# Seven products for a fourth pair of every gate, up and odd block, with the small dependent steps held together among the weights' parts

## The chip, the cores and the metric

The kernel runs on one core of a Trainium2 chip. The metric is the device time of one execution in microseconds (us). The engines are TensorE (PE: matmuls, and PEld for its weight loads), VectorE (DVE), ScalarE (ACT), GpSimd (POOL) and SyncE (SP, which issues the DMAs here).

## The reference

One layer of a streaming encoder on 256 tokens of width 2048, in float32, with a hidden width of 5632 in the two feed-forward networks (FFN):

```python
x = x + 0.5 * swiglu(rms_norm(x, ffn1_norm), ffn1_w_gate, ffn1_w_up, ffn1_w_down)
h = rms_norm(x, mix_norm);  proj = h @ w_in
x = x + concat(pool_mixer(...), gla_mixer(...)) @ w_out
x = x + mem_cross_attention(rms_norm(x, xattn_norm), rms_norm(mem, mem_norm), w_q, w_kv, w_o)
x = x + 0.5 * swiglu(rms_norm(x, ffn2_norm), ffn2_w_gate, ffn2_w_up, ffn2_w_down)
return rms_norm(x, final_norm)
# swiglu(h, wg, wu, wd) = (silu(h @ wg) * (h @ wu)) @ wd
```

All weights are read once, so their stream sets the order of all work. The change is to the gate and up products of the two FFNs, and to small steps around them.

## The kernel before, in words

**Units.** The weights come in units of 1 MB, 256 rows by 1024 columns, which is four quarters of 128 x 512 side by side on the partitions. A matmul runs in a fast form of float32 that keeps only part of the mantissa, so each operand is split in two, hi and lo, and a product is three matmuls: hi x hi, hi x lo, lo x hi (`products`, L323). For a unit that means: its DMA lands in one of three `raw` buffers; ScalarE casts it to hi, `wh` (L241); VectorE subtracts to get lo, `wl` (L242); TensorE does 2 token halves x 4 quarters x 3 = 24 matmuls of 128 x 512 into PSUM. This is a *plain* unit.

**Sevens.** A unit that takes part as a 2 x 2 block of a Strassen-like scheme is a *seven*: seven products instead of eight, 21 matmuls (`seven`, L448). VectorE first makes three sums of quarters in a tile `T`, which has one buffer (`add_weights`, L417: one instruction of 1024 columns and two of 512); then the raw quarters 1 to 3 are split into `xh` and `xl` (two buffers each), and T into `wh` and `wl` (three). The token side needs sums too: `Sums.make` adds up x or y parts of a pair of k-tiles in four short steps (L380 to L392) and splits the results (L247 on ScalarE, L248 on VectorE). With `over=True` one of the four sums replaces a part of the activations that nothing else reads, and three are extra.

**Blocks.** `block_s` goes through eight units of 2048 rows for 1024 columns of gate or up. Four PSUM tiles, all that there are, hold its seven sums and the plain quarters. Behind the last seven `combine` (L504 on ScalarE, L505, L506, L509 on VectorE) adds up the product parts of two tiles; behind the last unit `join(1)` and `join(0)` (L518) add the other two. The gate's result goes through SiLU on ScalarE; up's is multiplied in by VectorE (`ev_up`, L774, four instructions per block pair), three units later; eight transposes per half and a split (`turn`, L779 to L787, with PSUM tile `ph`) put the product into `ys`, the input of down. `turn` comes `CLEAR` units after the pair.

**Order.** An FFN is cut into parts `FF_PARTS`: 4, 4 and 3 columns of blocks, in pairs gate and up (the third part's last block has half gate, half up, "odd"), and a product down after each part. FFN 1's first gate block is a `block_t`, all plain units; that leaves ten `block_s` per FFN. Before, three of the eight units of each are sevens: `PAIRS = (0, 2, 4)`, in order 0 to 7. Some down units and those of the two output projections are sevens as well (`Y_PAIRS`), which stays.

`Stream` (L34 to L90) keeps a list of units and of steps between them; `st.op(f, n)` puts a step behind n more units. `emit` prepares the weights AHEAD = 2 units before TensorE's use: for each unit first the *next* unit's T sums (`prepare`), then this unit's split, then the reload of its raw buffer. Within an engine the tile framework chooses the order by a schedule made when the kernel is built; `in_turn` binds the weights' parts to one another in the order they are written, `latest` being the last one on ScalarE and VectorE, and `behind_weights` (L235) lets a step come no earlier than the latest part. A step placed so may still slide behind many later weights' parts.

**Small steps that the change touches.** At the start, x comes in eight chunks, whose transposes (L645) and splits lie between the first units' products (`amid_first`, L653); their squares (`x_squares`) give the norm's factor, `finish_norm` (L261). The memory's norm `mem_norm` (L1139) squares 16 pieces of the memory on ScalarE (L257) at the end of the first output projection, where `fold` (L702) transposes x anew and splits it (L218, L219).

Of the kernel before, what the change touches and what calls it, by code (L numbers as in the profile page):

```python
# [33 lines left out]
class Stream:  # L34
# [30 lines left out]
    def emit(self, load, prepare, split):  # L65
        done, w, late = -1, {}, []
        for u, f in self.items:
            if u is None:
                f()
                continue  # L70
            ahead = min(u, 1) if u < self.FIRST else self.AHEAD
            while done < min(u + ahead, len(self.units) - 1):
                done += 1
                while late:
                    late.pop(0)()
                if done + 1 < len(self.units):
                    prepare(done + 1, self.units[done + 1][2])
                w[done], rest = split(done, self.units[done][1])

                def finish(done=done, rest=rest):  # L80
                    if rest:
                        rest()
                    if done + self.RAW < len(self.units):
                        load(done + self.RAW)

                if rest:
                    late.append(finish)
                else:
                    finish()
            f(*w.pop(u))  # L90


def build(ctx, tc, I, out):
# [97 lines left out]
    def rsqrt(dst, sums, n, w):  # L191
# [14 lines left out]
        nc.vector.reciprocal(out=dst, in_=v)  # L206

# [27 lines left out]
    def behind_weights(f):  # L235

        with tc.issue_after(latest["vector"].ins), tc.issue_after(latest["scalar"].ins):
            f()

# [6 lines left out]
    def split(hi, lo, src):  # L246
        nc.scalar.copy(hi, src)  # L247
        nc.vector.tensor_tensor(out=lo, in0=src, in1=f32(hi), op=ALU.subtract)  # L248

# [11 lines left out]
    def finish_norm(n, spread_too=True):  # L261

        nc.vector.tensor_reduce(out=sums, in_=ss[:, :, :n], axis=AX.X, op=ALU.add)
        rsqrt(Rcol, sums, D, 2)
        if spread_too:
            diag["R"] = [diagonal(Rcol[:, t : t + 1]) for t in range(2)]

    def spread_norm():
# [96 lines left out]
    class Sums:  # L365
# [6 lines left out]
        def make(self, g):  # L372
# [19 lines left out]
            nc.vector.tensor_tensor(out=p12, in0=p12, in1=p22, op=ALU.add)  # L392
            split(self.tile[:, i, 0], self.tile[:, i, 1], a[:, 4 - n :])
            if self.over:
                split(act[:, 2 * g, 0, P:], act[:, 2 * g, 1, P:], p11)

# [55 lines left out]
    def block_s(srcs, act, sums, order, evict, merge=None, sevens=None):  # L452
# [47 lines left out]
        def combine():  # L500
# [7 lines left out]
            )  # L508
            nc.vector.tensor_tensor(out=e[:, 3], in0=b[:, 1], in1=e[:, 1], op=ALU.add)  # L509
            if merge is not None:  # L510
                merge(e[:, 2:4], e[:, 0:2])

        def join(j):
# [9 lines left out]
        for g in order:  # L523
            if g in sevens:
                st.unit(srcs[g], unit_s(g), split_seven, add_weights)
                if g == sevens[-1]:
                    st.op(combine)
            else:
                st.unit(srcs[g], unit_p(g))
# [123 lines left out]
    def amid_first(u):  # L653

        for c in ((1,), (2, 3))[u] if u < 2 else (u + 2,):
            if c < 8:
# [46 lines left out]
    def fold(c, gain):  # L703
# [43 lines left out]

    PAIRS = (0, 2, 4)
    CLEAR = PAIRS[-1] + 2

    def ffn(wg, wu, wd, down, amid=None):
        gate = {}
        x_sums = Sums("xe", xs, PAIRS, False)

# [33 lines left out]

        for i, g in enumerate(PAIRS):
            st.op(lambda g=g: behind_weights(lambda: x_sums.make(g)), (5, 7, 8)[i])  # L790
        for lo, n in FF_PARTS:
            whole = n == KT // 4
            for b in range(0, n - 1, 2):
# [7 lines left out]
                block_s(wwide(wu, n0), xs, x_sums, range(8), up.__setitem__)  # L801
                st.op(lambda held=held: held.update(gate))
# [6 lines left out]
            if n % 2:  # L809
                def both(j, c):  # L810
# [3 lines left out]
                    else:  # L814
                        ev_up(0, c)
                block_s(wtwo(wu, wg, (lo + n - 1) * NB), xs, x_sums, range(8), both)
                st.op(lambda n=n: turn(gate[0], 4 * (n - 1)), 1)
# [343 lines left out]
    st.op(mem_in, 2)  # L1161
    st.op(mem_norm, 6)

# [296 lines left out]
```

## Time and profile before

| what | us |
|---|---|
| three runs | 2126.57, 2127.61, 2129.54 (median 2127.61) |
| profiled execution, whole | 2126.7 |
| its span, first to last instruction | 2124.9 |
| matmul time of TensorE in it | 2102.9 |
| VectorE | 1615.6 |
| ScalarE | 1064.0 |

The mean granted clock of TensorE is 0.996 of full speed. In the views, L448 is a seven's line, L323 a plain product's; a row of waits has engine, tile and line, then what it waited for, the sum in us, the number of times and the longest; a row of windows has, for each engine, busy us and the number of instructions, then the granted clock, the DMA engines' share and GB/s; a row of a timeline has start, length, engine, line, operation, tiles and, in brackets, idle time before and who ended it; a row of a group ends in its count, busy us and mean ns, and idle time before it.

### The profile page before, as it was taken

The numbers are of one execution on the slowest core, as the hardware profiler recorded it, in microseconds if no ns is written. First come the engines' busy times: TensorE is split into PE (matmuls) and PEld (weight loads), VectorE is DVE, ScalarE is ACT, GpSimd is POOL, SyncE is SP. The second block draws the span as 40 slices with busy tenths as digits, with TensorE's granted clock in tenths as the row PEclk, the third lists the DMA queues.
The fourth block names the chain that finished last, engine by engine and source line by source line (L and its number), as shares of the span: only waits on it lengthen the run. The fifth ranks groups of instructions, "written<-read, shape, count | busy, mean of one in ns | idle before, by whom it ended". The sixth has DMA issues, their size and how long they took to land.

```text
span 2124.9 us, 24308 instructions
## 1 busy us (share of the span) xinstructions
PE 2102.9 (99%) x9972; PEld 1760.2 (83%) x9972; DVE 1615.6 (76%) x1438; ACT 1064.0 (50%) x954; POOL 14.0 (1%) x40
## 2 busy tenths in 40 slices
PE   9899999999999999999999999999999999999998
PEld 7788888888888888888888888888888888888886
DVE  6797889878885676678656555868978889788864
ACT  6554445544544546455645434555544555445444
POOL 0000000000000000000000000000000000000001
PEclk9999999999999999999999999999999999999999
DMA  7456665566656655557755455655567665676573
GB/s 275 162 198 218 231 222 201 198 212 244 215 201 236 221 165 182 170 173 240 251 189 178 158 159 165 232 201 196 198 219 237 218 202 195 218 237 218 200 256 118
DMA packets 143607, 435.94 MB, mean 205 GB/s; under 512 B 9860, under 2 KB 13544, under 8 KB 143112
## 3 DMA queue, kind: packets, MB, share of 16 engines
q1 hardware_dynamic: 143464, 434.38, 60.5%
q8 instruction: 78, 1.28, 0.2%
q14 instruction: 33, 0.27, 0.0%
q10 hardware_dynamic: 32, 0.01, 0.0%
HBM read 417.58 MB, written 16.78 MB: 204 GB/s over the span
## 4 chain that ended last, share of the span: by engine, by line
PE 96%; ACT 1%; DMA 1%; DVE 1%; issue 1%; SPq 0%; DVEq 0%; ACTq 0%
PE pt L323 51%; PE pt L448 17%; PE pa L308 14%; PE pb L323 6%; PE pe L323 3%; PE ph L784 1%; PE pl L1191 1%; PE pv L1226 1%; ACT wh L241 1%; DMA raw<-in_xattn_w_q 0%; DVE wl L242 0%; DMA x<-in_x 0%; PE px L709 0%; PE pp L910 0%; DMA raw<-in_ffn_w_up 0%
## 5 line engine op out<-in xcount | busy, mean ns | idle before, releaser
L242 DVE TENSOR_TENSOR wl<-raw,wh 128x2048 fp32r<-128x2048 f32 (+2 forms) x304 | 684.8, 2254 | 339.4 <-ACT wh L241 338.7
L241 ACT CAST wh<-raw 128x2048 fp32r<-128x2048 f32 (+2 forms) x304 | 572.5, 1884 | 613.2 <-PE pt L323 340.4
L323 PE MATMUL pt<-wh,xs 128*128 128x512 f32 x1856 | 589.6, 391 | 0.6 <-ACT xs L218 0.6
L323 PE MATMUL pt<-wh,ys 128*128 128x512 f32 x1440 | 449.2, 390 | 0.0
L323 PEld LDWEIGHTS pt<-wh,xs 128*128 128x128 f32 x1856 | 348.8, 188 | 73.0 <-ACT xs L218 1.0
L323 PE MATMUL pt<-wl,xs 128*128 128x512 f32 x928 | 362.3, 390 | 0.0
L308 PE MATMUL pa<-xs,wh 128*128 128x512 f32 x896 | 317.5, 398 | 3.3 <-DVE xs L219 3.3
L323 PEld LDWEIGHTS pt<-wh,ys 128*128 128x128 f32 x1440 | 269.9, 188 | 55.7
L323 PE MATMUL pt<-wl,ys 128*128 128x512 f32 x720 | 280.3, 389 | 0.0
L308 PE MATMUL pa<-xs,wl 128*128 128x256 f32 x896 | 249.2, 281 | 0.0
L241 ACT CAST wh<-T 128x2048 fp32r<-128x2048 f32 x78 | 149.4, 1915 | 132.4 <-PE pt L323 86.6
L323 PEld LDWEIGHTS pt<-wl,xs 128*128 128x128 f32 x928 | 174.6, 188 | 35.8
L308 PEld LDWEIGHTS pa<-xs,wh 128*128 128x128 f32 x896 | 168.1, 188 | 42.2 <-DVE xs L219 3.9
L242 DVE TENSOR_TENSOR wl<-T,wh 128x2048 fp32r<-128x2048 f32 x78 | 178.3, 2286 | 29.6 <-ACT wh L241 29.4
L308 PEld LDWEIGHTS pa<-xs,wl 128*128 128x128 f32 x896 | 169.7, 189 | 1.6 <-issue 0.2
L323 PEld LDWEIGHTS pt<-wl,ys 128*128 128x128 f32 x720 | 135.1, 188 | 28.0
L242 DVE TENSOR_TENSOR xl<-raw,xh 128x1536 fp32r<-128x1536 f32 x78 | 136.6, 1751 | 16.4 <-ACT xh L241 16.4
L241 ACT CAST xh<-raw 128x1536 fp32r<-128x1536 f32 x78 | 115.3, 1478 | 61.8 <-PE pt L448 49.7
L448 PE MATMUL pt<-wh,xe 128*128 128x512 f32 x360 | 125.0, 394 | 4.9 <-ACT xe L247 4.9
L323 PE MATMUL pb<-wh,xs 128*128 128x512 f32 x384 | 121.5, 392 | 0.0
L417 DVE TENSOR_TENSOR T<-raw 128x1024 f32<-128x1024 f32 x78 | 95.4, 1223 | 20.6 <-DMA raw<-in_ffn_w_gate 10.0
L417 DVE TENSOR_TENSOR T<-T,raw 128x512 f32<-128x512 f32 x156 | 107.3, 688 | 3.2
(230 smaller groups left out, 2079.7 us busy)
## 6 DMA issues: line engine op xcount, KB each, us to landing
raw<-in_ffn_w_down SPq DMA_DIRECT2D x88, 1024.0 KB, 5.6
raw<-in_ffn_w_up SPq DMA_DIRECT2D x80, 1024.0 KB, 5.7
raw<-in_ffn_w_gate SPq DMA_DIRECT2D x77, 1024.0 KB, 5.1
raw<-in_w_in SPq DMA_DIRECT2D x32, 1024.0 KB, 5.3
raw<-in_xattn_w_kv SPq DMA_DIRECT2D x32, 1024.0 KB, 5.2
raw<-in_w_out SPq DMA_DIRECT2D x16, 1024.0 KB, 5.5
raw<-in_xattn_w_q SPq DMA_DIRECT2D x16, 1024.0 KB, 5.1
raw<-in_xattn_w_o SPq DMA_DIRECT2D x16, 1024.0 KB, 5.5
```

The source lines that it names most:

```text
L241: in_turn("scalar", lambda: nc.scalar.copy(hi, src))
L242: in_turn("vector", lambda: nc.vector.tensor_tensor(out=lo, in0=src, in1=f32(hi), op=ALU.subtract))
L308: nc.tensor.matmul(o, w, x, start=k == 0 and i == 0, stop=last and i == 1)
L323: nc.tensor.matmul(ps, a, w, start=first and i == 0, stop=last and i == 2)
L417: in_turn("vector", lambda: nc.vector.tensor_tensor(out=o, in0=a, in1=b, op=ALU.add))
L448: nc.tensor.matmul(banks[n], x, w, start=n in fresh and j == 0, stop=n in ends and j == 2)
L784: nc.tensor.transpose(v[:, i, h * P : (h + 1) * P], g[:, h, i * P : (i + 1) * P], ident)
L1191: nc.tensor.matmul(ps[:, t, :M], ys[:, 4 * h + d, a, tok], xa["K"][:, d, b, :], start=i == 0, stop=i == 11,)
L1226: nc.tensor.matmul(ps[:, d, :S], xa["V"][:, m, a, col], xa["PT"][:, m, b, :], start=i == 0, stop=i == 5,)
```

## The change

- `PAIRS` becomes (0, 2, 4, 6) and the order of units in every `block_s` 0, 1, 2, 3, 4, 6, 5, 7: four sevens, four plain units, two sevens one behind another. The sums for x are made with `over=True`.
- `emit` splits a seven before it prepares the next unit, if that is a seven too, since T has one buffer.
- `among_weights` is new: it runs a step behind the latest parts and makes the step's own last instructions the latest, so that later parts of weights come behind the step. It is used for the combine, both kinds of token sums, the fold's splits and the first norm's factor.
- The x sums come 5, 7, 9 and 10 units in; `CLEAR` goes from 6 to 7.
- The start has four more spare transposes behind x chunk 0, x chunk 3 one unit later, and the norm's factor one unit earlier, with a square root and a SiLU on ScalarE around it. `turn_gains` of the later gains moves from unit 22 to 35.
- The memory's squares are spread over four units, all behind the weights' parts, and its factor comes at unit 7.

```diff
@@ emit
-                if done + 1 < len(self.units):
-                    prepare(done + 1, self.units[done + 1][2])
+                after = self.units[done + 1][2] if done + 1 < len(self.units) else None
+                both = after and self.units[done][2]
+                if not both:
+                    prepare(done + 1, after)
                 w[done], rest = split(done, self.units[done][1])
+                if both:
+                    prepare(done + 1, after)
@@
+    def among_weights(f):
+        scalar, vector = behind_weights(f)
+        latest["vector"] = vector
+        if scalar is not None:
+            latest["scalar"] = scalar
@@ block_s
-                    st.op(combine)
+                    st.op(combine if merge else lambda: among_weights(combine))
@@ amid_first
-        for c in ((1,), (2, 3))[u] if u < 2 else (u + 2,):
+        for c in ((1,), (2,), (3, 4))[u] if u < 3 else (u + 2,):
@@ fold
-        for j in range(4):
-            split_scaled(xs, 4 * c + j, v[:, j, :], gcol(gain + 4 * c + j))
+        def parts():
+            for j in range(4):
+                done = split_scaled(xs, 4 * c + j, v[:, j, :], gcol(gain + 4 * c + j))
+            return done
+
+        among_weights(parts)
@@ make_y_sums
-            st.op(lambda g=g: behind_weights(lambda: y_sums.make(g)), after)
+            st.op(lambda g=g: among_weights(lambda: y_sums.make(g)), after)
@@ ffn
-    PAIRS = (0, 2, 4)
-    CLEAR = PAIRS[-1] + 2
+    PAIRS, ORDER = (0, 2, 4, 6), (0, 1, 2, 3, 4, 6, 5, 7)
+    CLEAR = 7
-        x_sums = Sums("xe", xs, PAIRS, False)
+        x_sums = Sums("xe", xs, PAIRS, True)
-            st.op(lambda g=g: behind_weights(lambda: x_sums.make(g)), (5, 7, 8)[i])
+            st.op(lambda g=g: among_weights(lambda: x_sums.make(g)), (5, 7, 9, 10)[i])
@@ the three calls of block_s, alike
-                    block_s(wwide(wg, n0), xs, x_sums, range(8), lambda j, c: ev_gate(j, c, 0))
+                    block_s(wwide(wg, n0), xs, x_sums, ORDER, lambda j, c: ev_gate(j, c, 0))
@@ the start
     st.op(lambda: x_chunk(0))
+    st.op(lambda: spare_transposes(4))
-    st.op(lambda: finish_norm(8, False), 7)
+    def first_factor():
+        nc.scalar.activation(chain[:, 1, 0:2], invc[:, 0:2], AF.Sqrt)
+        done = finish_norm(8, False)
+        return nc.scalar.activation(sums, Rcol, AF.Silu), done
+
+    st.op(lambda: among_weights(first_factor), 6)
-    st.op(lambda: turn_gains(G_MIX, G_END), 22)
+    st.op(lambda: turn_gains(G_MIX, G_END), 35)
@@ the memory
+    def mem_squares(lo, hi):
+        for c in range(lo, hi):
+            row_squares([xa[f"mem{h}"][:, c * S : (c + 1) * S] for h in range(2)], c)
+
     def mem_norm():
-        for c in range(8):
-            row_squares([xa[f"mem{h}"][:, c * S : (c + 1) * S] for h in range(2)], c)
-    st.op(mem_norm, 6)
+    for c in range(4):
+        st.op(lambda c=c: behind_weights(lambda: mem_squares(2 * c, 2 * c + 2)), c + 3)
+    st.op(lambda: behind_weights(mem_norm), 7)
```

Helper functions otherwise only return their last instructions.

More of the change, by code (lines that the diff above doesn't have):

```diff
@@ L205, in rsqrt @@
             nc.vector.tensor_tensor(out=v, in0=v, in1=r, op=ALU.add)
-        nc.vector.reciprocal(out=dst, in_=v)
+        return nc.vector.reciprocal(out=dst, in_=v)
     def diagonal(col):
@@ L237, in behind_weights @@
         with tc.issue_after(latest["vector"].ins), tc.issue_after(latest["scalar"].ins):
-            f()
+            return f()
+    def among_weights(f):
[3 more added lines that the diff above has]
+            latest["scalar"] = scalar
     def split_weights(hi, lo, src):
@@ L246, in split @@
     def split(hi, lo, src):
-        nc.scalar.copy(hi, src)
-        nc.vector.tensor_tensor(out=lo, in0=src, in1=f32(hi), op=ALU.subtract)
+        high = nc.scalar.copy(hi, src)
+        return high, nc.vector.tensor_tensor(out=lo, in0=src, in1=f32(hi), op=ALU.subtract)
     def split_pair(dst, kt, src):
@@ L263, in finish_norm @@
         nc.vector.tensor_reduce(out=sums, in_=ss[:, :, :n], axis=AX.X, op=ALU.add)
-        rsqrt(Rcol, sums, D, 2)
+        done = rsqrt(Rcol, sums, D, 2)
         if spread_too:
             diag["R"] = [diagonal(Rcol[:, t : t + 1]) for t in range(2)]
+        return done
     def spread_norm():
@@ L392, in make @@
             nc.vector.tensor_tensor(out=p12, in0=p12, in1=p22, op=ALU.add)
-            split(self.tile[:, i, 0], self.tile[:, i, 1], a[:, 4 - n :])
+            done = split(self.tile[:, i, 0], self.tile[:, i, 1], a[:, 4 - n :])
             if self.over:
-                split(act[:, 2 * g, 0, P:], act[:, 2 * g, 1, P:], p11)
+                done = split(act[:, 2 * g, 0, P:], act[:, 2 * g, 1, P:], p11)
+            return done
         def parts(self, g):
@@ L508, in combine @@
             )
-            nc.vector.tensor_tensor(out=e[:, 3], in0=b[:, 1], in1=e[:, 1], op=ALU.add)
+            last = nc.vector.tensor_tensor(out=e[:, 3], in0=b[:, 1], in1=e[:, 1], op=ALU.add)
             if merge is not None:
                 merge(e[:, 2:4], e[:, 0:2])
+            return None, last
         def join(j):
@@ L711, in fold @@
                 )
-        for j in range(4):
-            split_scaled(xs, 4 * c + j, v[:, j, :], gcol(gain + 4 * c + j))
+        def parts():
+            for j in range(4):
+                done = split_scaled(xs, 4 * c + j, v[:, j, :], gcol(gain + 4 * c + j))
+            return done
+        among_weights(parts)
         for h in range(2):
@@ L797, in ffn @@
                 else:
-                    block_s(wwide(wg, n0), xs, x_sums, range(8), lambda j, c: ev_gate(j, c, 0))
+                    block_s(wwide(wg, n0), xs, x_sums, ORDER, lambda j, c: ev_gate(j, c, 0))
                 held, up = {}, {}
                 into_down = whole and b
-                block_s(wwide(wu, n0), xs, x_sums, range(8), up.__setitem__)
+                block_s(wwide(wu, n0), xs, x_sums, ORDER, up.__setitem__)
                 st.op(lambda held=held: held.update(gate))
@@ L815, in both @@
                         ev_up(0, c)
-                block_s(wtwo(wu, wg, (lo + n - 1) * NB), xs, x_sums, range(8), both)
+                block_s(wtwo(wu, wg, (lo + n - 1) * NB), xs, x_sums, ORDER, both)
                 st.op(lambda n=n: turn(gate[0], 4 * (n - 1)), 1)
```

## Prediction

> **What bounds the kernel now.** First the page: the busy shares and the chain that ended last.
>
> ```profile
> PE 2102.9 (99%) x9972; PEld 1760.2 (83%) x9972; DVE 1615.6 (76%) x1438; ACT 1064.0 (50%) x954; POOL 14.0 (1%) x40
> PE 96%; ACT 1%; DMA 1%; DVE 1%; issue 1%; SPq 0%; DVEq 0%; ACTq 0%
> ```
>
> TensorE (PE) is busy for 99% of the span and carries 96% of the chain, so removed matmuls come off the time, as long as nothing else becomes late. The second row of reading is TensorE's waits, since they are all that is left besides matmuls:
>
> ```profile
> PE pt L448 <- ACT xe L247: 4.9, 1, 4.9
> PE pa L308 <- DVE xs L219: 3.3, 2, 2.8
> ...
> PE pt L448 <- DVE xl L242: 1.2, 1, 1.2
> PE px L645 <- DMA x<-in_x: 0.7, 1, 0.7
> ```
>
> Each is one event, not a steady loss. All blocks of gate and up after the start run without a gap, which the windows over two blocks with three sevens each, and over the down product that follows them two blocks later, show:
>
> ```profile
> core 0: us, PE busy (x) PEld busy (x) DVE busy (x) ACT busy (x) POOL busy (x), PEclk, DMA share, GB/s
> 320.39:361.87 41.48, 41.48 (x184) 34.35 (x183) 36.38 (x27) 22.16 (x16) 0.00 (x0) 1.00 0.58 203
> 361.87:405.17 43.30, 43.30 (x200) 36.01 (x199) 39.54 (x32) 23.29 (x16) 0.00 (x0) 1.00 0.56 195
> ...
> 446.65:533.42 86.77, 86.77 (x393) 72.08 (x391) 75.93 (x68) 41.88 (x29) 0.00 (x0) 1.00 0.66 230
> ```
>
> The reader is to see how near VectorE (DVE) stands: 36.38 of 41.48 us, and 39.54 of 43.30 us in the block that holds 16 turning transposes (200 PE instructions, not 184).
>
> **The removed products.** The pace of a product comes from the chain of waits:
>
> ```profile
> 470.34 4.76 PE pt L448 x21
> 475.10 27.20 PE pt L323 x120
> ```
>
> 27.20 / 120 = 0.2267 us. A plain unit has 24 products, 5.44 us; a seven has 21, 4.76 us. The change makes one more seven in each of 10 blocks per FFN, two FFNs: 20 x 3 = 60 products, 60 x 0.2267 = **-13.6 us**. The Trainium skill (TensorE: Matmul & The Clock Gate, Back-to-back issue gap) has 215.7 ns for 512 columns; by that figure it would be 12.9 us, and the measured pace decides.
>
> **What each new seven costs VectorE.** Its instructions one behind another, in the timeline around the boundary at 361.87:
>
> ```profile
> 349.44 2.28 DVE L242 TENSOR_TENSOR wl<-raw,wh 128x2048 fp32r<-128x2048 f32 x1
> 351.64 1.75 DVE L242 TENSOR_TENSOR xl<-raw,xh 128x1536 fp32r<-128x1536 f32 x1
> 353.31 0.68 DVE L509 TENSOR_TENSOR sg<-pt,sg 128x512 f32<-128x512 f32 x1
> 353.91 2.28 DVE L242 TENSOR_TENSOR wl<-T,wh 128x2048 fp32r<-128x2048 f32 x1
> 356.77 1.22 DVE L417 TENSOR_TENSOR T<-raw 128x1024 f32<-128x1024 f32 x1 [0.57 <-DMA raw<-in_ffn_w_gate]
> 358.02 1.42 DVE L417 TENSOR_TENSOR T<-T,raw 128x512 f32<-128x512 f32 x2
> 359.36 2.28 DVE L242 TENSOR_TENSOR wl<-raw,wh 128x2048 fp32r<-128x2048 f32 x1
> 361.56 1.22 DVE L518 TENSOR_TENSOR sg<-pt,sg 128x1024 f32<-128x1024 f32 x1
> 362.70 1.75 DVE L242 TENSOR_TENSOR xl<-raw,xh 128x1536 fp32r<-128x1536 f32 x1
> 364.36 1.22 DVE L518 TENSOR_TENSOR sg<-pt,sg 128x1024 f32<-128x1024 f32 x1
> 365.50 2.28 DVE L242 TENSOR_TENSOR wl<-T,wh 128x2048 fp32r<-128x2048 f32 x1
> ```
>
> By distance of starts: wl 2.20 (349.44 to 351.64), xl 1.67, the three sums T 2.59 (356.77 to 359.36), a join 1.14 (361.56 to 362.70). A seven takes 2.59 + 1.67 + 2.21 = 6.47 us of VectorE, a plain unit 2.2: each change of one into the other adds 4.27 us to VectorE and takes 0.68 us from TensorE. For the pair of blocks quoted: VectorE 36.38 + 39.54 + 2 x 4.27 = **84.5 us**, TensorE 41.48 + 43.30 - 2 x 0.68 = **83.4 us**. VectorE has more to do than TensorE in such a pair, where it now has 9 us to spare. In down it keeps 11 us of room (75.93 of 86.77), so a debt never passes from one run of four blocks to the next.
>
> VectorE also waits. A raw buffer is loaded again once its unit is split: above, wl ends at 349.44 + 2.28 = 351.72, and T can start on the reloaded buffer at 356.77, **5.05 us** later. The new order 0, 1, 2, 3, 4, 6, 5, 7 puts fewer instructions between that release and the sum that reads the reload. For the third seven they are xl 1.67 and wl 2.21, 3.88 us: VectorE waits about 1.2 us. For the first seven of the next block, behind two sevens in a row, only the second one's wl and a plain wl, 4.41 us: about 0.65 us.
>
> **Where that reaches TensorE.** The static order of the changed kernel differs at the block boundary. Before, the wl of the new block's second unit (359.36 above) stands ahead of both joins. In the changed kernel it stands behind join 1, the next T's first sum, join 0 and the rest of T; where a turn falls, behind its two ys splits too. Join 0 waits for TensorE's last product. The two further durations:
>
> ```profile
> L774 DVE SCALAR_TENSOR_TENSOR sg<-sg,Rcol,sg 128x512 f32<-128x512 f32 x40 | 27.3, 745 | 0.0
> L248 DVE TENSOR_TENSOR ys<-ph,ys 128x1024 fp32r<-128x1024 f32 x22 | 26.0, 1217 | 4.4 <-ACT ys L247 4.4
> ```
>
> I follow one block with a turn, from where TensorE starts its sixth unit, the second of two sevens in a row (time 0), and let that unit's xl be ready just then. Its nine products of plain parts last 2.04 us, so its wl (2.2) just holds. VectorE: wl of the sixth 2.2, of the seventh 4.4; T of the next block's first unit waits for its buffer until 5.05 and ends at 7.65; wl of the eighth 9.85; the combine (0.6 + 1.14 + 0.6 and a wait for ScalarE, about 2.5) 12.35; xl 14.0, wl 16.2; join 1 17.35; first T sum 18.5; ys 19.65; join 0 20.8; ys 21.9; rest of T 23.25; wl of the second unit **25.45**. TensorE: 4.76 + 2 x 5.44 + 1.8 for the transposes (43.30 - 41.48) = 17.44 for the block's end. The next unit's first PSUM tile is the one join 1 frees (17.35, in time); seven products on, at 19.05, it needs the tile that the first ys split frees: 0.65 us lost. Then join 0's tile is in time; at 22.5 it wants the wl of 25.45, or 0.2 us after: 2.8 us. Together about 3.5, with a semaphore's way for each 3.7 us. Without the debt ahead (buffers landing in time) only the last part is left: end + 0.25 + 1.14 (join 0) + 1.13 (ys) + 1.34 + 2.2 = 6.06 against 4.76 + 0.4 us of cover: 0.9.
>
> There are two such boundaries per FFN (into the up block of the second pair of each run of four): 4 x 3.7 = 14.8 us, lower end 4 x 0.9 = 3.6. In three blocks per FFN the four evictions of L774, 4 x 0.66 = 2.65 us by their starts, stand ahead of the sixth unit's xl: by the same walk it is late by 0.7 us, 6 x 0.7 = 4.2, lower end nothing. I take 14.8 + 4.2 = **+19.0 us**, between 3.6 and 22 (3 us more if the boundaries without a turn lose a little each as well: end + 0.25 + 1.14 + 1.34 + 2.2 = 4.93 stands against 4.76 + 0.2 there). I take the long value because the refill of 5.05 us is a row of this trace and the list is fixed.
>
> **What the small steps give back.** Three waits now stand in the trace; first the clock beside them.
>
> ```profile
> 13.84:17.26 3.42, 2.76 (x17) 2.05 (x17) 3.42 (x4) 3.33 (x8) 0.00 (x0) 1.00 1.11 357
> ...
> 58.22:61.63 3.41, 1.53 (x6) 0.63 (x4) 3.41 (x5) 0.06 (x1) 0.00 (x0) 1.00 0.60 179
> 61.63:65.04 3.41, 0.00 (x0) 0.00 (x0) 2.57 (x5) 0.00 (x0) 0.00 (x0) 0.50 0.98 372
> 65.04:68.46 3.42, 2.60 (x6) 2.12 (x7) 3.30 (x9) 3.24 (x5) 0.00 (x0) 0.50 0.16 63
> 68.46:71.87 3.41, 3.41 (x9) 2.64 (x9) 1.24 (x3) 1.59 (x3) 0.00 (x0) 0.50 0.00 0
> ...
> 1037.84:1041.25 3.41, 0.74 (x4) 0.66 (x5) 2.98 (x4) 3.31 (x14) 0.00 (x0) 1.00 0.19 14
> 1041.25:1044.67 3.42, 3.42 (x14) 3.03 (x13) 1.67 (x9) 2.61 (x4) 0.00 (x0) 0.50 0.79 293
> ```
>
> *FFN 1's start.* The rows of token sums come from the groups by line:
>
> ```profile
> L380 DVE TENSOR_TENSOR j<-xs 128x512 f32<-128x512 f32 x6 | 4.1, 684 | 0.0
> ...
> L387 DVE TENSOR_TENSOR j<-j 128x128 f32<-128x128 f32 x18 | 5.2, 286 | 0.2
> ```
>
> One pair's sums are one instruction of the first kind and four short ones (0.68 + 4 x 0.29 = 1.8 us) with their splits behind. Now the waits: 1.2 (xl) and 4.9 us (the token sums, xe), then about 6.0 us at clock 0.50 until 71.87, 3.0 lost: 9.1 us. The sums are now issued as a group among the weights' parts, and a fourth pair's is added, while VectorE has one seven more per block there as well. So the gain lies between nothing and 9.1; neither end is nearer by a row, I take the middle, **-4.6**.
>
> *The memory's norm.* 2.8 us of wait near 1040, and a window of 3.42 us at 0.50 in which its 14 instructions, four of them short ones, would have taken about 2.0 at the pace of full clock: 2.8 + 1.4 = 4.2 us. There the 16 squares of the memory stand on ScalarE between the fold's splits; in the changed kernel's order the splits come together ahead of the squares, which are spread over four units. **-4.2**, at worst nothing.
>
> *The second x chunk.* It waits 0.7 us for its data; one chunk now comes a unit later: **-0.7**, at worst nothing. The other steps cost nothing I can find: four more spare transposes stand where TensorE waits for x anyway; two table loads and the gains' turning are on ScalarE (50% busy) or three short matmuls; without that cover they would cost some 1 us.
>
> **Sum.** -13.6 + 19.0 - 4.6 - 4.2 - 0.7 = -4.1 us. The durations come from the profiled execution of 2126.7 us, which lies 0.9 below the median of 2127.6: 2122.6 on its scale, **2123.5 us** on the median's.
>
> **Rivals.**
> *A, VectorE keeps up.* Debt does not build: the reload lands within 3.9 us when the sum needs it, and boundaries cost 0.9 each. Then -13.6 + 3.6 - 4.6 - 4.2 - 0.7 = -19.5: 2108.1. For it: the DMA queue is at a 0.56 to 0.66 share only. Against it: 5.05 us above, in the same stretch.
> *B, the clock falls at the four turn boundaries; slower.* The longest piece there is 2.8 us of idle. A window of 3.41 us with 1.53 or 0.74 busy was followed by one at 0.50 (58.22, 1037.84); one with 2.76 busy was not (13.84). If the piece falls in one window, 0.6 is busy and the next is at half pace: 1.7 us lost, and as at 65.04 to 71.87 a second one, 3.4. Four times 2.55 on average is +10.2: -4.1 + 10.2 = +6.1, 2133.7. It decides from about 1.9 us of idle within one window; a piece that a window's edge cuts in halves leaves 2.0 busy in each, between the two cases that the rows show. The Trainium skill (TensorE: Matmul & The Clock Gate, Part 1) lets the rate fall only after a whole idle window of about 3.4 us: by that rule 2.8 us would never do it and B would be worth nothing. The wait of 2.8 us near 1040, which is followed by 0.50, speaks against the rule.
> *C, the start keeps its stall.* The fourth pair's sums and seven eat what the grouping gives: -4.1 + 4.6 = +0.5, 2128.1, no change.
>
> **How the numbers follow.** Forecast 0.38, A 0.30, B 0.23, C 0.09. Bounds of the unknown terms around the forecast reach 2119 to 2129; with A below (its gain at the start full: 2104) and B above (one window each at 1.7: 2130; two each: 2137) the range is **2104 to 2136**. A measurement tells 0.2%, 4.3 us, from no change. Faster: A 0.30 and just over half of the forecast case, 0.20, together 0.50; same: the forecast's rest 0.17, C 0.07, B's edge 0.01, together 0.25; slower: B 0.22, C 0.02, forecast 0.01, together 0.25.
>
> **What would show it.** PE instructions on the page 9972 - 60 + 4 = 9916. In the windows of a gate and up pair DVE near its limit (over 95%) and PE below it. In TensorE's waits a new row <- DVE wl L242 at products of plain units, two long ones per FFN of 2 to 3 us, and smaller ones <- DVE ys and xl; no row for xe over 1 us; none of 2.8 us at L308. A mean clock under 0.996 speaks for B; PE waits below 6 us in all for A. The prediction is wrong if the weights' reload is faster than 5 us in the new order, or if stalls come in every block and not at the turns alone.

## The result and the profile after

The changed kernel takes 2140.18 us (median of 4 runs, 2138.35 to 2141.02) against 2127.53 us of the kernel before: 1.006 times as long, 95% interval 1.0047 to 1.0073. It is 12.7 us slower; 4.0 us faster was forecast. The profiled execution took 2141.0 us, its span is 2138.9 (before 2126.7 and 2124.9). From the page, busy time and the chain:

```profile
PE 2099.3 (98%) x9916; PEld 1746.6 (82%) x9916; DVE 1707.2 (80%) x1538; ACT 1092.8 (51%) x986; POOL 14.1 (1%) x40
PE 69%; DVE 19%; DMA 6%; issue 3%; ACT 3%; SPq 0%; DVEq 0%; ACTq 0%
```

TensorE has the 56 instructions less that were counted, but it carries 69% of the chain, not 96%: VectorE now has 19% of it and the DMAs 6%. TensorE's waits, largest first:

```profile
PE pt L462 <- ACT wh L253: 17.6, 14, 2.2
PE pt L462 <- DVE xs L223: 2.0, 2, 1.8
PE pt L462 <- DVE xl L254: 1.9, 5, 0.7
```

The first row, 14 waits and 17.6 us, is for the hi part of a seven, which ScalarE casts when VectorE's sums are ready. (L462 is the seven's line now; before it was L448, and lines further on have moved likewise.) No wait is left at L321, the memory's norm.

Where the time went shows best stage by stage, in the one profiled execution that each kernel has. Below, a stage lasts from TensorE's first product in it to the first of the next one; the columns are the difference to the kernel before in us, for the changed kernel and for four of the experiments told below.

| stage (length before) | changed | fold_free | three_pairs | four_only | three_fold |
|---|---|---|---|---|---|
| FFN 1, gate and up, first run with the start (186.1) | -1.4 | -2.1 | -5.2 | -2.1 | -4.8 |
| second run of four blocks (167.7) | +3.2 | +3.2 | 0.0 | +2.1 | 0.0 |
| third run of three blocks (126.3) | -0.6 | -0.5 | -0.1 | -1.0 | -0.1 |
| mixer's projection (205.2) | -0.7 | +0.5 | -0.3 | +0.4 | +0.5 |
| first output projection (87.4) | **+6.2** | +0.6 | +6.1 | -0.1 | +0.5 |
| attention with the memory's norm (299.8) | -4.7 | -4.0 | -4.4 | +1.2 | -4.0 |
| second output projection (89.7) | **+4.4** | 0.0 | +4.3 | 0.0 | 0.0 |
| FFN 2, gate and up, first run (171.6) | **+5.2** | +4.3 | 0.0 | +3.0 | 0.0 |
| second run (167.7) | +2.3 | +2.6 | -0.1 | +0.9 | -0.1 |
| third run (126.3) | +0.1 | -0.3 | -0.1 | 0.0 | -0.1 |

The down products are within 0.7 us everywhere. Of a run's 2.0 to 2.7 us of removed products (0.68 for each added seven) nothing, or little, is left in any run of gate and up, and the output projections, in which no product was added or removed, lost 10.5 us.

**Inside a run of gate and up.** The four blocks of FFN 1's second run, by windows from block start to block start:

```profile
core 0: us, PE busy (x) PEld busy (x) DVE busy (x) ACT busy (x) POOL busy (x), PEclk, DMA share, GB/s
277.65:318.60 40.95, 40.95 (x182) 33.93 (x181) 38.28 (x28) 22.15 (x14) 0.00 (x0) 1.00 0.66 227
318.60:359.25 40.65, 40.65 (x182) 33.64 (x180) 37.38 (x28) 23.16 (x17) 0.00 (x0) 1.00 0.56 188
359.25:404.38 45.13, 43.39 (x197) 35.06 (x195) 42.67 (x35) 22.07 (x15) 0.00 (x0) 1.00 0.56 191
404.38:448.54 44.16, 41.83 (x182) 33.75 (x181) 40.29 (x29) 22.39 (x17) 0.00 (x0) 1.00 0.58 207
```

The first two blocks run without a gap and keep their gain (40.95 and 40.65, not 41.48). The third and the fourth have TensorE's gaps, and VectorE at 95% and 91% of the time. VectorE falls behind by block; down sets it right. It is not overloaded on the whole: in the four blocks it is busy for 158.6 us, where TensorE's products and transposes need 165.0 (four times 180 products at 0.2267 us, and 1.8), and in the third and fourth block for 83.0, where TensorE needs 83.4. It is late because its list is fixed and it has to stand idle in it, for 12.3 of the 170.9 us, 7.9 of them for reloads. The boundary at 404.38, where a turn falls, on VectorE:

```profile
385.72 1.75 DVE L254 TENSOR_TENSOR xl<-raw,xh 128x1536 fp32r<-128x1536 f32 x1
...
392.64 1.22 DVE L431 TENSOR_TENSOR T<-raw 128x1024 f32<-128x1024 f32 x1 [0.78 <-DMA raw<-in_ffn_w_up]
...
401.69 2.28 DVE L254 TENSOR_TENSOR wl<-T,wh 128x2048 fp32r<-128x2048 f32 x1
403.89 1.22 DVE L533 TENSOR_TENSOR sg<-pt,sg 128x1024 f32<-128x1024 f32 x1
405.03 1.21 DVE L431 TENSOR_TENSOR T<-raw 128x1024 f32<-128x1024 f32 x1
406.16 1.22 DVE L260 TENSOR_TENSOR ys<-ph,ys 128x1024 fp32r<-128x1024 f32 x1
407.29 1.21 DVE L533 TENSOR_TENSOR sg<-pt,sg 128x1024 f32<-128x1024 f32 x1
408.43 1.21 DVE L260 TENSOR_TENSOR ys<-ph,ys 128x1024 fp32r<-128x1024 f32 x1
409.56 1.41 DVE L431 TENSOR_TENSOR T<-T,raw 128x512 f32<-128x512 f32 x2
410.88 2.28 DVE L254 TENSOR_TENSOR wl<-raw,wh 128x2048 fp32r<-128x2048 f32 x1
```

and what TensorE makes of it:

```profile
404.15 0.48 PE L336 MATMUL pt<-wh,xs 128*128 128x512 f32 x1
405.25 0.47 PE L462 MATMUL pt<-xh,xs 128*128 128x512 f32 x1 [0.63 <-DVE sg L533]
...
407.43 0.50 PE L462 MATMUL pt<-wh,xs 128*128 128x512 f32 x1 [0.32 <-DVE ys L260]
...
413.00 0.50 PE L462 MATMUL pt<-wh,xs 128*128 128x512 f32 x1 [1.39 <-ACT wh L253]
```

The reader sees the forecast walk: the sums wait for the reload, join 1 starts when TensorE is at its last products, and from there VectorE does seven things in a row, until 413.2, before the second unit can go on. By starts of products the three waits are 0.88 + 0.49 + 1.55 = 2.92 us (forecast 3.5 to 3.7). Waits in the brackets are shorter than these gaps, since a product's modelled end reaches into them. The last is booked on ScalarE's cast, which follows the rest of T at 410.97, a product that stands ahead of the plain unit's in TensorE's list; the plain unit's wl is ready in the same moment.

The boundary before it has no turn, and it had been given 0.2 us at most:

```profile
357.26 2.28 DVE L254 TENSOR_TENSOR wl<-T,wh 128x2048 fp32r<-128x2048 f32 x1
359.47 1.22 DVE L533 TENSOR_TENSOR sg<-pt,sg 128x1024 f32<-128x1024 f32 x1
360.60 1.21 DVE L431 TENSOR_TENSOR T<-raw 128x1024 f32<-128x1024 f32 x1
361.73 1.22 DVE L533 TENSOR_TENSOR sg<-pt,sg 128x1024 f32<-128x1024 f32 x1
362.87 1.41 DVE L431 TENSOR_TENSOR T<-T,raw 128x512 f32<-128x512 f32 x2
364.19 2.28 DVE L254 TENSOR_TENSOR wl<-raw,wh 128x2048 fp32r<-128x2048 f32 x1
```

TensorE is done with the block at 359.25. Join 0 could start then; it starts at 361.73, because VectorE is still at the first unit's wl (until 359.5) and then at join 1 and a sum. TensorE stands still for 1.65 us after 364.46.

**In the output projections.** VectorE in the first one of the changed kernel:

```profile
981.31 2.28 DVE L254 TENSOR_TENSOR wl<-T,wh 128x2048 fp32r<-128x2048 f32 x1
987.70 0.48 DVE L223 SCALAR_TENSOR_TENSOR xs<-px,gains,xs 128x256 fp32r<-128x256 f32 x1 [4.11 <-ACT xs L222]
988.73 0.49 DVE L223 SCALAR_TENSOR_TENSOR xs<-px,gains,xs 128x256 fp32r<-128x256 f32 x1 [0.54 <-ACT xs L222]
...
994.25 0.48 DVE L223 SCALAR_TENSOR_TENSOR xs<-px,gains,xs 128x256 fp32r<-128x256 f32 x1 [0.54 <-ACT xs L222]
994.65 1.22 DVE L431 TENSOR_TENSOR T<-raw 128x1024 f32<-128x1024 f32 x1
```

and in the kernel before:

```profile
978.60 2.28 DVE L242 TENSOR_TENSOR wl<-T,wh 128x2048 fp32r<-128x2048 f32 x1
980.91 1.23 DVE L417 TENSOR_TENSOR T<-raw 128x1024 f32<-128x1024 f32 x1
982.17 1.42 DVE L417 TENSOR_TENSOR T<-T,raw 128x512 f32<-128x512 f32 x2
983.51 2.29 DVE L242 TENSOR_TENSOR wl<-raw,wh 128x2048 fp32r<-128x2048 f32 x1
985.71 0.48 DVE L219 SCALAR_TENSOR_TENSOR xs<-px,gains,xs 128x256 fp32r<-128x256 f32 x1
```

Before, the next sums and a plain part are made first, and the fold's splits of x come when their transposes are there. In the changed kernel the next sums are bound behind the eight splits. VectorE stands still for 4.1 us until the first one's transposes are done, and then takes about 1.03 us a split, in turn with ScalarE (987.70 to 988.73), so that T starts at 994.65, 11 us after the wl before it has ended, and TensorE runs dry. Behind the waits follows a window of 3.41 us at half rate in each projection (from 1000.3 and 1389.4 us, last section); eight products in it start 0.43 us apart and not 0.23, so that 3.2 of the 10.5 us are the clock's.

### The profile page after: what moved, and what is told of

Its sections match the earlier page's. It is cut to its first block, busy times and chain, and to the rows that moved or that the text cites. A ratio compares the mean times of both kernels' runs of the same rounds, so it can differ in the third digit from the quotient of the medians.

```text
span 2138.9 us, 24386 instructions
## 1 busy us (share of the span) xinstructions
PE 2099.3 (98%) x9916; PEld 1746.6 (82%) x9916; DVE 1707.2 (80%) x1538; ACT 1092.8 (51%) x986; POOL 14.1 (1%) x40
## 4 chain that ended last, share of the span: by engine, by line
PE 69%; DVE 19%; DMA 6%; issue 3%; ACT 3%; SPq 0%; DVEq 0%; ACTq 0%
PE pt L336 32%; PE pa L321 15%; PE pt L462 9%; DVE wl L254 7%; PE pb L336 6%; DVE T L431 5%; PE pe L336 3%; DMA raw<-in_ffn_w_gate 3%; DMA raw<-in_ffn_w_up 2%; DVE xl L254 2%; ACT wh L253 2%; DVE sg L533 1%; DVE sg L520 1%; DVE sg L793 1%; PE pl L1221 1%
## 5 line engine op out<-in xcount | busy, mean ns | idle before, releaser
L254 DVE TENSOR_TENSOR wl<-raw,wh 128x2048 fp32r<-128x2048 f32 (+2 forms) x284 | 637.9, 2250 | 251.7 <-ACT wh L253 251.1
L253 ACT CAST wh<-raw 128x2048 fp32r<-128x2048 f32 (+2 forms) x284 | 532.4, 1881 | 411.1 <-PE pt L336 216.6
L336 PE MATMUL pt<-wh,xs 128*128 128x512 f32 x1536 | 496.7, 392 | 0.0
L336 PEld LDWEIGHTS pt<-wh,xs 128*128 128x128 f32 x1536 | 288.8, 188 | 59.5 <-ACT wh L253 0.2
L321 PE MATMUL pa<-xs,wh 128*128 128x512 f32 x896 | 315.9, 397 | 0.0
L253 ACT CAST wh<-T 128x2048 fp32r<-128x2048 f32 x98 | 187.5, 1913 | 227.3 <-DVE T L431 186.9
L336 PE MATMUL pt<-wl,xs 128*128 128x512 f32 x768 | 300.8, 392 | 1.1 <-DVE wl L254 1.1
L321 PE MATMUL pa<-xs,wl 128*128 128x256 f32 x896 | 248.5, 281 | 0.0
L254 DVE TENSOR_TENSOR wl<-T,wh 128x2048 fp32r<-128x2048 f32 x98 | 224.0, 2286 | 13.5 <-ACT wh L253 13.2
L321 PEld LDWEIGHTS pa<-xs,wh 128*128 128x128 f32 x896 | 167.6, 188 | 38.1 <-issue 0.3
L253 ACT CAST xh<-raw 128x1536 fp32r<-128x1536 f32 x98 | 145.1, 1480 | 97.9 <-DMA raw<-in_ffn_w_gate 52.7
L254 DVE TENSOR_TENSOR xl<-raw,xh 128x1536 fp32r<-128x1536 f32 x98 | 171.5, 1750 | 5.0 <-ACT xh L253 5.0
L336 PEld LDWEIGHTS pt<-wl,xs 128*128 128x128 f32 x768 | 144.8, 189 | 31.7 <-DVE wl L254 2.0
L321 PEld LDWEIGHTS pa<-xs,wl 128*128 128x128 f32 x896 | 169.1, 189 | 1.7 <-issue 0.2
L462 PE MATMUL pt<-wh,xs 128*128 128x512 f32 x320 | 126.4, 395 | 16.2 <-ACT wh L253 14.9
L462 PE MATMUL pt<-wh,xe 128*128 128x512 f32 x320 | 123.2, 389 | 0.0
```

The source lines that it names most:

```text
L253: in_turn("scalar", lambda: nc.scalar.copy(hi, src))
L254: in_turn("vector", lambda: nc.vector.tensor_tensor(out=lo, in0=src, in1=f32(hi), op=ALU.subtract))
L321: nc.tensor.matmul(o, w, x, start=k == 0 and i == 0, stop=last and i == 1)
L336: nc.tensor.matmul(ps, a, w, start=first and i == 0, stop=last and i == 2)
L462: nc.tensor.matmul(banks[n], x, w, start=n in fresh and j == 0, stop=n in ends and j == 2)
```

## The experiments

They ran beside the kernel before, whose median was 2126.0 to 2126.7 us in the three groups; each ratio has its 95% interval.

**1. The fold's splits.** `fold_free` is the changed kernel with one edit:

```diff
-        among_weights(parts)     # fold
+        parts()
```

> The changed kernel, but the fold's eight splits of x are plain again and bind no weights' part behind them. Theory F (the splits, which wait for the transposes and then alternate between ScalarE and VectorE at 1.03 us a step, hold the next weights' parts back by about 11 us at both output projections): the two projections lose their 6.2 and 4.4 us against the kernel before, 2140.2 - 10.5 = 2129.7, perhaps plus up to 4.2 if the wait at the memory's norm comes back. Rival Y (the token sums of y, bound in the same way, are what holds them): no change, 2140. Either way the gate and up stretches stay as they are, about 8.6 us longer in all than before.

Measured: 2131.67 us, 1.0025 (1.0015 to 1.0034). The projections lose 5.6 of 6.2 and all of 4.4 us, the gain at the memory's norm stays, and gate and up change by 1.4 us in all. Theory F holds within 2 us.

**2. The sums of y.**

```diff
-            st.op(lambda g=g: among_weights(lambda: y_sums.make(g)), after)
+            st.op(lambda g=g: behind_weights(lambda: y_sums.make(g)), after)
```

> The changed kernel, but the token sums of y bind no weights' part behind them, as before the change. Theory F: no change within 1.5 us of 2140. Rival Y: the output projections lose their 10.5 us, 2129.7.

Measured: 2135.33 us, 1.0043 (1.0028 to 1.0058): between the two. The first projection gains 3.1 us, the second nothing. So the bound sums of y have a part in the first projection's loss, on top of the splits; at the second the splits alone do it. Of the 3.1 us some 1.6 are the clock, since the window at half rate is missing in the first projection here, and the rest are shorter waits. This is the least sure of the measurements: four runs, three between 2134.5 and 2136.1 and one at 2140.4.

**3. Three pairs again, all small steps as changed.**

```diff
-    PAIRS, ORDER = (0, 2, 4, 6), (0, 1, 2, 3, 4, 6, 5, 7)
-    CLEAR = 7
+    PAIRS, ORDER = (0, 2, 4), tuple(range(8))
+    CLEAR = 6
-        x_sums = Sums("xe", xs, PAIRS, True)
+        x_sums = Sums("xe", xs, PAIRS, False)
```

and the sums again at 5, 7 and 8.

> The changed kernel with three sevens per block again in the order 0 to 7, turns 6 units later and sums as before; all small steps stay as changed. If four sevens are too many for VectorE (theory V): gate and up run without waits as before the change, so the time is the kernel before plus 10.5 us at the output projections, minus 4.7 at the memory's norm and minus 0.7 at the second projection, plus what the start changes (0 to -5): 2128 to 2133. Rival G (the grouping of the combine and the sums causes the waits in gate and up): the waits stay and the saving of 13.6 us goes, about 2150.

Measured: 2127.55 us, 1.0003 (0.9993 to 1.0013), just under the 2128 to 2133 that were expected. Gate and up are back within 0.1 us of the kernel before in all five runs behind the start; the start itself is 5.2 us shorter. The fourth pair makes the waits there (V), and the small steps make those at the projections.

**4. The fourth pair alone.** The kernel before with `PAIRS`, `ORDER`, `CLEAR`, the sums' places and `emit` of the changed one; no `among_weights`.

> The kernel before with only the fourth pair: pairs 0, 2, 4, 6, the new order, sums made in place, turns 7 units later, the split ahead of the next sums between two sevens; no step is bound among the weights' parts, and the start and the memory's norm are as before. Theory V: the same waits in gate and up as in the changed kernel, output projections as before: 2127.5 + 8.7 = 2136, give or take 4. Rival G: no new waits in gate and up, 2127.5 - 13.6 = 2114.

Measured: 2132.16 us, 1.0025 (1.0015 to 1.0035). V in kind, at the lower end of what was expected: 60 products fewer, and slower. Gate and up are 3.0 us over the kernel before in all; in `fold_free` it is 7.2. So the grouping costs some 4 us there: experiment 9.

**5. Both edits, 1 and 3: three pairs, plain fold.**

> Three sevens per block in the order 0 to 7 with the small steps as changed, but the fold's splits plain. If the two causes add (four sevens in gate and up; the fold's splits bound at the projections), only the gains are left: about 5.2 us at the start, 4.0 at the memory's norm, 0.3 elsewhere, less 0.5 at the second projection: 2126.5 - 9 = 2117.5. Rival: the gain at the memory's norm needs the bound splits, then 2121.5.

Measured: 2118.85 us, 0.9964 (0.995 to 0.9978), faster than both kernels. The two causes add: experiments 1 and 3 took 8.5 and 12.6 us off 2140.2, which makes 2119.1. The gain at the memory's norm does not need the bound splits. TensorE's largest waits are now

```profile
PE pt L462 <- ACT wh L253: 3.8, 3, 1.9
PE pt L336 <- DVE wl L254: 2.6, 1, 2.6
```

and all of these lie in the first 80 us.

**6. Turns earlier.** `fold_free` with `CLEAR = 5`.

> The changed kernel with the fold's splits plain (2131.7 us) and the turns 5 units behind the pair, not 7, so that their two splits of ys stand away from the block's end. Theory T (the ys splits between the joins are what makes the wait at those four boundaries long, 2.9 us each): these fall to the 0.5 to 1.6 us of the boundaries without a turn, 2131.7 - 6.5 = 2125. Rival L (VectorE has too much to do in the pair as a whole, wherever the splits stand): the waits move, 2131.7 within 2 us.

Measured: 2131.72 us, 1.0027 (1.0017 to 1.0036), no change. But it decides nothing: the ys splits stand where they stood, one between the joins and one behind them (405.54 and 407.80 us, join 0 at 406.67). By the program the turn's transposes need the PSUM tile that the combine frees, so an earlier place can't move them ahead of it; in the trace they run from 401.4 us on, and the combine ends at 399.5.

**7. The even order.** `fold_free` with `ORDER = (0, 1, 2, 3, 4, 5, 6, 7)`, four sevens.

> The changed kernel with the fold's splits plain and the four sevens in the order 0 to 7, each followed by a plain unit. Theory R (the reload of a raw buffer, 5.05 us, against 3.88 us of work between its release and the next sums): every seven now waits about 1.2 us on its DMA, four times a block, not once or twice, and VectorE has no room for it: 10 to 40 us longer, 2142 to 2172, with VectorE's waits for the weights' DMA at least doubled from the 32 us of the changed kernel. Rival: the pair of sevens in a row is what makes TensorE wait, and the even order is better: under 2128.

Measured: 2155.26 us, 1.0135 (1.0121 to 1.015). R holds: 23.6 us longer. VectorE's waits for the weights in it

```profile
DVE T L431 <- DMA raw<-in_ffn_w_up: 31.0, 24, 1.6
DVE T L431 <- DMA raw<-in_ffn_w_gate: 27.4, 20, 2.3
```

are 58.4 us, where the changed kernel has

```profile
DVE T L431 <- DMA raw<-in_ffn_w_gate: 17.3, 15, 2.4
DVE T L431 <- DMA raw<-in_ffn_w_up: 15.0, 16, 1.5
```

32.3 us (`fold_free`, which differs in nothing but the order, 31.5): 1.8 times, a little under the doubling expected. Two sevens in a row are the better order here; that the second's work covers part of the reload is the count of the prediction.

**8. The sums of the weights on GpSimd.**

```diff
-            in_turn("vector", lambda: nc.vector.tensor_tensor(out=o, in0=a, in1=b, op=ALU.add))
+            in_turn("pool", lambda: nc.gpsimd.tensor_tensor(out=o, in0=a, in1=b, op=ALU.add))
```

> The changed kernel with the fold's splits plain and the sums T of the weights on GpSimd. It takes 2.6 us of each seven off VectorE: in a pair of blocks 84.5 - 8 x 2.6 = 63.7 us. Theory V (VectorE's load): the waits of gate and up go if GpSimd needs no more than about twice VectorE's time per sum: 2131.7 - 18 = 2114 or less. Rival P: GpSimd is over three times slower or slows VectorE beside it; T then comes too late at the two sevens in a row of every block, and the time grows by 2 to 10 us a block, 2170 to 2330.

Measured: 2277.08 us, 1.0705 (1.069 to 1.072), rival P. The sums take

```profile
L431 POOL TENSOR_TENSOR T<-T,raw 128x512 f32<-128x512 f32 x196 | 391.7, 1998 | 15.4
L431 POOL TENSOR_TENSOR T<-raw 128x1024 f32<-128x1024 f32 x98 | 335.4, 3422 | 1252.7 <-DMA raw<-in_xattn_w_o 353.6 <-DVE wl L254 313.0 <-DMA raw<-in_ffn_w_down 167.5
```

3.42 us and twice 2.00 on average, where VectorE needs 1.22 and twice 0.69: 2.8 times as long, 7.4 us ahead of each seven with one T buffer. The averages hide two cases. With VectorE idle beside them the sums take 2.39 and 1.26 us, and at the longest 4.47 and 3.25. The Trainium skill (GPSIMD Engine Reference, 4.1 Engine selection) has about twice for two inputs; the undisturbed sums agree. And VectorE is slowed in its turn, first here, then in `fold_free`:

```profile
L254 DVE TENSOR_TENSOR xl<-raw,xh 128x1536 fp32r<-128x1536 f32 x98 | 232.7, 2374 | 11.5 <-ACT xh L253 11.3
L254 DVE TENSOR_TENSOR xl<-raw,xh 128x1536 fp32r<-128x1536 f32 x98 | 171.5, 1750 | 17.9 <-ACT xh L253 17.9
```

An xl takes 1.75 us when no sum runs on GpSimd and up to 3.96 beside one, a plain wl up to 4.50 in place of 2.29. So of rival P the second half came true, GpSimd slowing VectorE, and not the three times. VectorE's load can't be moved there in this way, and the run leaves open how much of the waits in gate and up a lighter VectorE would save.

**9. The combine unbound.** `fold_free` with

```diff
-                    st.op(combine if merge else lambda: among_weights(combine))
+                    st.op(combine)
```

> The changed kernel with the fold's splits plain and the combine not bound among the weights' parts. If the binding of the combine is what makes gate and up of the changed kernel 4 us longer than those of the kernel with the fourth pair only: 2131.7 - 4 = 2127.7. Rival (the binding of the sums at the start, or the turns, makes the difference): 2131.7 within 1.5.

Measured: 2128.6 us, 1.0009 (1.0 to 1.0018): 3.1 of the 4 us. Unbound, the steps of the combine and the weights' parts mix: in the second run of FFN 1 the next first unit's xl (397.33 us) comes ahead of the combine's last step (399.00).

**10. Combine and sums of y unbound.**

> As the run with the combine unbound, and the token sums of y unbound too: the best that the fourth pair can do with these small steps. 2127 us; if it were under 2118.8, the fourth pair would pay after all.

Measured: 2129.25 us, 1.001 (1.0001 to 1.0019). That is 10.4 us over three pairs with the plain fold, so the fourth pair does not pay in any of the arrangements tried.

**11. Turns without VectorE.** `fold_free` with

```diff
-            split(ys[:, k : k + 4, 0, :], ys[:, k : k + 4, 1, :], v)
+            nc.scalar.copy(ys[:, k : k + 4, 0, :], v)
+            nc.scalar.copy(ys[:, k : k + 4, 1, :], v)
```

> The changed kernel with the fold's splits plain (2131.7 us), and in the turns the lo part of ys is written by ScalarE as a second copy of the hi part: the lo half of the products' left side in down is then not what it should be, the amount of matmul work is the same. VectorE loses two splits of 1.13 us between the joins at each of the four turn boundaries. Theory T (these splits make that wait long): the wait of 2.94 us there falls by 2 to 2.9, in all -8 to -11.6: 2120 to 2124. Rival L (VectorE's load in the pair is what counts): 2.3 us less out of an overload of about 1 us a pair plus waits; the boundaries without a turn, 0.5 to 1.6 us each, gain as well, beyond -11.6.

Measured: 2127.47 us, 0.9999 (0.999 to 1.0009): 4.2 us less, half of what T expected. The wait at the turn of FFN 1's second run falls from 2.9 to 1.55 us, and now TensorE waits for ScalarE's second copy there. The boundary without a turn ahead of it keeps its wait (1.5 us in `fold_free`, 1.4 here), which speaks against rival L. Theory T has the direction; how much the two splits alone cost stays open between 1.4 and 2.9 us a turn, since the copy brings a wait of its own. FFN 2's first run became 2.4 us longer: there the wait for the copy comes in one piece of 2.2 us (1539.5), and the next window runs at half rate (1541.9, 1.6 us). The profiled execution was the slowest of the ten, so the others may not have this.

**12. Only the sums of x bound.** The kernel before, with `among_weights` for `x_sums.make` and nothing else.

> The kernel before, and nothing but the token sums of x bound among the weights' parts. If that is where the 5 us at the start come from: 2126.3 - 5 = 2121.3. Rival (the chunks' order, the spare transposes and the earlier factor give them): 2126.3 within 1.5.

Measured: 2123.19 us, 0.9984 (0.9975 to 0.9994). The start is 3.5 us shorter, so most of the start's gain is these sums (three pairs with all small steps have 4.8 and 5.2 there); a further 1.5 us came at the memory's norm, by the clock (below).

## Why the prediction was wrong

Two steps failed. The boundaries without a turn were taken to cost nothing, and cost 7.9 us; the fold's splits, bound among the weights' parts, were taken to cost nothing, and cost 9.9. Term by term:

- **Products, -13.6.** Right: 60 fewer, at the same pace; the first two blocks of FFN 1's second run show 0.5 and 0.8 us less.
- **Waits in gate and up, +19.0, at most 22.** Too small: about 28. That is the six runs' sum in the table, +8.7, plus the 13.6 that were removed, plus 5.8 gained in the first 92 us (the 331st product of weights starts at 90.9 us, before at 96.7).
  - At the four turns the walk was right: 2.9 us in three of them and 2.3 in the other, 11.1 in all, where 14.8 was taken. It has a slip besides: 17.44 + 0.65 + 4.76 is 22.85 and not 22.5, so that it should have come to 3.1 to 3.3, which is nearer still.
  - The **step that failed** is the boundaries without a turn: "end + 0.25 + 1.14 + 1.34 + 2.2 = 4.93 stands against 4.76 + 0.2 there". This lets join 0 start when TensorE ends. The walk for the turns starts with VectorE's debt, this one without it, though both are boundaries of the same run. With the debt the same list gives 15.64 us for the block's end, wl of the first unit at 16.2, join 1 at 17.35, the first sum 18.5, join 0 19.65, the rest of T 21.0, wl 23.2 against 20.8 (15.64 + 4.76, and 0.4 of cover as at a turn): 2.4 us. The runs show 2.4 (105.8 us), 1.65 (364.5), 0.5 (622.1), 2.1 (1507), 0.9 (1766) and 0.35 (2023), 7.9 us in all; 0.8 more came two units behind the one at 1507 (1520), and 1.6 through the clock behind the first (109.4). The prediction had named stalls outside the turns as a sign of being wrong.
  - The late xl behind the evictions, for which 4.2 was taken, is five waits of 0.3 to 0.5 us, 2.0 in all. What is left of the 28 us is 1.0 at the start of FFN 2's last down (2061.4), about 0.1 behind each wait, since the second product after one starts 0.33 us after the first and not 0.23 (366.34 and 366.67), and smaller pieces.
  - VectorE's load came out a little smaller than the 84.5 us of the sum: 83.0 in the third and fourth block, just under TensorE's 83.4. So "more to do than TensorE" did not hold; what holds is the order and its waits. Experiments 3 and 4 show that the fourth pair makes these waits; that it does so by the order and the reloads and not by the load alone is argued, for no experiment separates the two.
- **The start, -4.6.** Right in size: behind the first block the changed kernel gains 4.3 us. The kernel of experiment 12 gains 4.0 in the same stretch, so the bound sums give most of it. **The memory's norm, -4.2:** right (-4.7, and -4.0 with the plain fold). **The x chunk, -0.7:** TensorE still waits 0.7 us for x, now at 8 us, and yet the first block is 1.5 us shorter. Half of that is there by the 13th product: before, products start 0.43 us apart until 10.5 us, now only until 7.1. The four spare transposes, which the prediction took for filling, keep TensorE busy for all of 3.60 to 7.02 us (before for 2.86 us); that they do it was not tried alone.
- **"The other steps cost nothing I can find."** This is the **other step that failed**, and the largest: the fold's bound splits cost 9.9 of the 10.5 us that the two projections lost (experiment 1). The prediction saw that these splits come together on ScalarE and booked that as a gain for the memory's norm. It did not ask, for VectorE, what is queued behind a bound step and what the step itself waits for: here the next weights' sums, behind eight steps that wait for transposes. Why successive splits alternate at 1.03 us, when the unbound ones go in pairs in the same time, is only argued: in the bound order four splits of one PSUM tile follow one another, in the other the two tiles take turns. It was not tried by itself.
- **Rival B** did not happen at the turns: their waits come in three pieces, and the clock stayed at 1.00. It fell at three other places, 1.6 us each: 109.4, 1000.3 and 1389.4 us. **Rival A** did not happen either: the reload took its 5 us in the new order too (the second seven's xl releases its buffer at 387.47, the sums that read the reload start at 392.64, 5.2 us later). In **rival C** the start would have kept its stall; it did not.

With the measured terms the sum is -13.6 + 28.0 - 5.8 - 4.7 + 10.5 = +14.4 us, and 0.5 less in the other stages, as between the two spans (14.0). These terms are read from the stages of the two traces and so must add up to it; that the causes are the right ones rests on experiments 1 and 3 to 5.

## What to carry to other kernels

Binding a small step among the stream's parts puts everything behind it in line with whatever the step waits for: ask of each bound step what ends its own wait, and don't bind steps that wait for the very engine that the stream feeds. When work is moved from a bound engine to one with 10% of room, work the load out as a debt that passes from block to block, and give every boundary behind the first the same debt. What pays may be the small steps and not the change that they were meant for: three pairs with the plain fold are 0.36% faster than the kernel before.

## What the runs showed of the clock

In these traces half rate comes in windows of 3.41 us: before the change three in a row from 61.63 us and one from 1041.25. A window need not be idle for the next one to be at half rate, and one that was idle for 1.5 us did not bring it about. In the changed kernel:

```profile
106.03:109.44 3.41, 1.17 (x5) 0.90 (x5) 3.41 (x3) 2.98 (x2) 0.00 (x0) 1.00 0.00 0
109.44:112.86 3.42, 3.42 (x10) 2.65 (x9) 2.98 (x2) 0.73 (x1) 0.00 (x0) 0.50 0.91 292
...
997.00:1000.40 3.40, 1.60 (x5) 1.05 (x6) 3.40 (x3) 3.40 (x3) 0.00 (x0) 0.99 0.00 0
1000.40:1003.80 3.40, 3.40 (x10) 2.68 (x9) 3.40 (x3) 0.66 (x1) 0.00 (x0) 0.51 0.93 239
```

1.17 and 1.60 us busy: the next window is at half. In the kernel with only the sums of x bound (experiment 12) the memory's norm has a wait of 2.9 us, like the one before the change (2.8), but a window's edge cuts it:

```profile
1032.06:1035.47 3.41, 2.11 (x12) 1.55 (x11) 1.70 (x2) 3.38 (x8) 0.00 (x0) 1.00 0.04 16
1035.47:1038.89 3.42, 1.87 (x12) 1.69 (x13) 2.32 (x6) 2.88 (x13) 0.00 (x0) 1.00 0.44 111
1038.89:1042.30 3.41, 3.41 (x22) 3.00 (x21) 3.21 (x7) 1.86 (x2) 0.00 (x0) 1.00 0.50 196
```

2.11 and 1.87 us busy, and no half rate: the stage is 1.5 us shorter. In the other runs a window with 1.71 us busy was followed by half rate (experiment 9, 59.13 us) and one with 1.72 was not (experiment 1, 57.81); but three with 1.58 to 1.66 were not either (experiment 8, 131.61, 135.02 and 653.84). So the limit lies near half a window, and the busy time that the trace gives, in which the ends of products are modelled, does not settle it more closely. The Trainium skill (TensorE: Matmul & The Clock Gate, Part 1) asks for a whole idle window; the runs do not agree.
